# Hybrid encoder block on one core: w_out's second parts on VectorE, a slot table for each choice, and weight splits and the last normed row in other places around the last tile's routing

## The chip, the core and the metric

The kernel runs as one program on one core of a Trainium2 chip. The metric is the device time of one execution in microseconds (us); several executions are timed and their median is taken. The engines of a core are TensorE (PE in the profile, its weight loads PEld), VectorE (DVE), ScalarE (ACT), GpSimd (POOL) and SyncE (SP), each with an instruction queue that runs in order. Engines wait for one another and for DMA transfers through semaphores. DMA is issued from SyncE in most places, from ScalarE in some, and indirect DMA (rows by a list of indices) from GpSimd.

## What is computed

One layer over 2048 tokens of width 1024, all in float32:

```python
h = rmsnorm(x, mix_norm_g)
z = h @ w_in                                   # 512 + 512 + 2 * 1024 columns
y_f = fourier_mix(z[:, :512]) @ w_fourier_out
y_s = glu(gelu(ssm_both_directions(z[:, 512:1024]))) @ w_ssm_out
gates = sigmoid(z[:, 1024:])
x = x + (gates[:, :1024] * y_f + gates[:, 1024:] * y_s) @ w_out
hn = rmsnorm(x, ffn_norm_g)
group  = top_1(softmax(hn @ wg + bg))          # of 8 groups
expert = top_2(hn @ we + be, inside group)     # of 8 experts in it
w      = p_group * softmax(the two logits)
x = x + sum over the 2 choices of w * (silu(hn @ w_gate[e]) * (hn @ w_up[e])) @ w_down[e]
out = rmsnorm(x, final_norm_g)
```

There are 64 experts with an inner width of 512; gate, up and down of one expert are 6 MB, read as six blocks of 1 MB.

## The kernel before

**Products in two parts.** A float32 product is made of three products of a shorter type. `split` (L50 to L54) writes a tensor as a high part, a ScalarE copy (L53), and a second part, the difference of the two, by default on VectorE (L54). `mm3` (L57 to L61) issues high by high, high by low and low by high into one PSUM tile.

**The stages.** First come the input norm and w_in, the Fourier and state-space branches and the gates (to about 735 us of the profile), then the mixing stage `stage_m` (to about 1131 us and, with the routing of the last tiles, to about 1180), then `stage_e` with the experts, `stage_o` for experts with more than 128 tokens (a loop of `tot` passes over a row list, `For_i(0, tot)`; with these inputs `tot` is 0) and `stage_z`.

**Order in the mixing stage.** The order of its instructions comes out of a list of due times. `unit(d, f)` emits PE work of planned length d, after all that has come due by then; `at(dt, f)` puts f on the list dt after the present planned time; `flush` empties the list. A step's place in an engine's queue is thus set by these numbers.

The stage has blocks of 256 tokens. For each block b it makes the GLU (`glu`, tile names pglu, yr, y_h, y_l), then `merge` (L1265 and on): for each of 8 feature blocks, PE forms `pso` (y_s @ w_ssm_out) in a PSUM pool of three buffers that the GLU shares; VectorE multiplies it by its gate and adds the Fourier part (L1273, L1274, into gt_l); ScalarE copies the result to mg_h, and VectorE subtracts into mg_l (L54). `out_half` then forms merged @ w_out for half a tile of 128 tokens (tile `po`) and adds it to x (L1305, x_l). `w_out` itself is loaded in six pieces, four of one 128-row slice and two of two slices (`places`, L1392), into buffers that are still unused (raw_hn, raw_hnT, two raw_x_l, raw_mg_h, raw_mg_l), and split at times of their own (L1395): ScalarE makes the high part, and the second part of five pieces is made by GpSimd, of the last (k = 6) by VectorE.

**Norm and routing of a tile.** `norm` has four steps: the sum of squares on ScalarE (L1324, whose product goes into a buffer of the tag hn), its mean and a power of −1/2 on GpSimd (L1331, tile inv), a refinement step on VectorE (L1334 to L1337), and n4, which makes the normed row hn on VectorE (L1341) and stores it on SyncE (L1342). For tile 15 n4 is kept as `last_norm` and called at the end. `turn` transposes x, `logits` multiplies by the router weights (L1371), L1381 scales that to lg, and `route` is a generator whose steps choose the group and experts with small VectorE instructions and two tanh on ScalarE (L1557 r_th, L1580 r_td).

**The slot table.** Each (token, choice) gets a row in a table `tab` in DRAM: slot within the expert times 64 plus the expert; the row holds token number and weight. `clear_table` (L1505) zeroes the table early, with eight issues on SyncE during the stage before. The route steps scatter the entries of tiles 0 to 13 by indirect DMA from GpSimd (L1626), one instruction per tile and choice; as they write one tensor, each waits until the one before has landed. `load_table` (L1655) reads the first 128 slots of every expert to `tbm`, early in the last tile's routing. Tiles 14 and 15 don't go through DRAM there: PE multiplies one-hot matrices (r_a, built from r_pos, and r_b) into `ptab`, in PSUM, and `moe_open` adds `ptab` to `tbm` (L1704), makes the indices `ix` (L1751) and issues the gathers of the first three experts' rows of hn from DRAM (L1755). Their scatters follow later, for the overflow loop.

**Weights of the experts.** Blocks of 1 MB go into a ring of raw buffers (seven, two more, and two more after the last tile, `moe_weights` and `moe_pairs`). `split_h(n)` makes block n's high part on ScalarE (L1690, w_h), `split_l(n)` its second part on VectorE (L1696, w_l); only then is the raw buffer free, and `load_more` issues the next loads. Before `moe_open`, blocks 0 to 3 get their high parts and block 0 its second part; `moe_open` makes the second parts of 1, 2 and 3 behind the gathers.

These are the lines of the last tiles:

```python
at(-1.9, self.split_h, 0)
at(0.0, self.split_l, 0)
rs[15] = route(15, 1)
at(1.1, self.split_h, 1)
...
self.flush()
for _ in range(3):
    rs[15]()
self.last_norm()
```

## Time and profile before

Three executions took 2399.49, 2400.45 and 2407.3 us; the median is 2400.45. The profiled execution took 2403.95 us, of which the span of the profile is 2402.1.

| | busy, us | share of the span | instructions |
|---|---|---|---|
| TensorE products (PE) | 2264.6 | 94% | 11770 |
| TensorE weight loads (PEld) | 1911.2 | 80% | 11770 |
| VectorE (DVE) | 1928.8 | 80% | 2720 |
| ScalarE (ACT) | 1378.8 | 57% | 1699 |
| GpSimd (POOL) | 428.3 | 18% | 364 |
| DMA | 630.96 MB | mean 263 GB/s | 201326 packets |

Shares are averages over stages of different kinds, so a stretch must be looked at by itself. In the views of the trace that follow, a row of the timeline holds the start in us from the beginning of the span, the duration, the engine, the line of the kernel, the operation and its tiles (out<-in), and in brackets how long the engine had been idle ahead of it and who ended that. A PE product of 512 columns takes about 0.39 us from start to end, but is pipelined with the next.

### The profile page before, as it was taken

What the parts mean: (1) busy time and instruction counts of PE and PEld (TensorE: products, weight loads), DVE (VectorE), ACT (ScalarE), POOL (GpSimd) and SP (SyncE); (2) the same over time, 40 slices, a digit from 0 to 9 for tenths busy, and PEclk for the clock granted to TensorE, in tenths of its full rate; (3) what the DMA queues carried; (4) which work ended last, traced back from release to release, by engine and by line L of the source; (5) the groups of instructions that cost most, each with busy time, mean ns of one, the idle gap of its engine ahead of it and who ended that gap; (6) DMA issues with size and microseconds to landing.
All of it is one profiled execution on the core that took longest, in us unless ns stands there. A gap on an engine that the chain in (4) does not pass through costs nothing.

```text
span 2402.1 us, 32307 instructions
## 1 busy us (share of the span) xinstructions
PE 2264.6 (94%) x11770; PEld 1911.2 (80%) x11770; DVE 1928.8 (80%) x2720; ACT 1378.8 (57%) x1699; POOL 428.3 (18%) x364
## 2 busy tenths in 40 slices
PE   6999899999999999999699997999999999999995
PEld 6997678887887899997588886888888887777773
DVE  7876779988964566566799997999999998888877
ACT  4443235545543222221488886888888877777773
POOL 2224500000001000111122121211212112211132
PEclk9999999999999999999799999999999999999998
DMA  5555644364436534435799997999999999999975
GB/s 198 185 185 198 243 150 144 95 205 153 136 103 197 171 106 140 133 103 209 269 357 377 387 377 306 396 373 380 373 382 381 374 371 372 374 373 375 370 282 203
DMA packets 201326, 630.96 MB, mean 263 GB/s; under 512 B 29065, under 2 KB 100747, under 8 KB 150476
## 3 DMA queue, kind: packets, MB, share of 16 engines
q1 hardware_dynamic: 173068, 578.27, 64.7%
q0 software_dynamic: 20912, 39.10, 6.2%
q10 hardware_dynamic: 7184, 11.51, 1.5%
q8 instruction: 93, 1.52, 0.2%
q14 instruction: 69, 0.57, 0.1%
HBM read 552.28 MB, written 109.58 MB: 276 GB/s over the span
## 4 chain that ended last, share of the span: by engine, by line
PE 34%; DMA 26%; DVE 20%; issue 13%; ACT 4%; POOL 2%; SPq 1%; DVEq 0%; POOLq 0%; ACTq 0%
DMA raw<-in_w_e 16%; DVE w_l L1696 9%; DMA x<-xg,ix 6%; PE pg L59 4%; PE pg L61 3%; PE pg L60 3%; PE po L59 2%; PE po L61 2%; PE po L60 2%; PE pso L60 1%; PE pso L61 1%; PE pso L59 1%; POOL oh L1987 1%; PE pl L1371 1%; ACT xg L1797 1%
## 5 line engine op out<-in xcount | busy, mean ns | idle before, releaser
L1696 DVE TENSOR_TENSOR w_l<-raw,w_h 128x2048 fp32r<-128x2048 f32 x384 | 862.3, 2284 | 22.8 <-ACT w_h L1690 22.3
L1690 ACT CAST w_h<-raw 128x2048 fp32r<-128x2048 f32 x384 | 732.6, 1913 | 246.7 <-DMA raw<-in_w_e 88.0
L59 PE MATMUL pgu<-w_h,xT_h 128*128 128x512 f32 x1024 | 407.2, 398 | 12.2 <-issue 12.2
L60 PE MATMUL pgu<-w_l,xT_h 128*128 128x512 f32 x1024 | 401.7, 392 | 9.5 <-DVE w_l L1696 9.5
L61 PE MATMUL pgu<-w_h,xT_l 128*128 128x512 f32 x1024 | 400.9, 392 | 0.0
L1761 POOL DMA_INDIRECT x<-xg,ix x62 | 99.2, 1600 | 890.7 <-ACT xg L1797 859.4
L60 PEld LDWEIGHTS pgu<-w_l,xT_h 128*128 128x128 f32 x1024 | 193.5, 189 | 54.2 <-DVE w_l L1696 15.8
L59 PEld LDWEIGHTS pgu<-w_h,xT_h 128*128 128x128 f32 x1024 | 193.4, 189 | 51.1 <-issue 12.4
L61 PEld LDWEIGHTS pgu<-w_h,xT_l 128*128 128x128 f32 x1024 | 192.8, 188 | 41.6 <-DVE xT_l L1773 0.2
L59 PE MATMUL pg<-hk_h,wg_h 128*128 128x512 f32 x512 | 207.1, 405 | 8.4 <-ACT gt_t L836 8.3
L59 PE MATMUL py<-w_h,aT_h 128*128 128x512 f32 x512 | 205.6, 402 | 1.9 <-ACT aT_h L1771 1.9
L61 PE MATMUL pg<-hk_h,wg_l 128*128 128x512 f32 x512 | 201.7, 394 | 1.9 <-DVE wg_l L54 1.9
L60 PE MATMUL pg<-hk_l,wg_h 128*128 128x512 f32 x512 | 201.3, 393 | 0.0
L61 PE MATMUL py<-w_h,aT_l 128*128 128x512 f32 x512 | 200.3, 391 | 0.4 <-DVE aT_l L1773 0.4
L60 PE MATMUL py<-w_l,aT_h 128*128 128x512 f32 x512 | 200.2, 391 | 0.0
L1773 DVE TENSOR_TENSOR aT_l<-pst,aT_h 128x512 fp32r<-128x512 f32 x64 | 44.3, 691 | 96.2 <-ACT aT_h L1771 96.2
L59 PEld LDWEIGHTS pg<-hk_h,wg_h 128*128 128x128 f32 x512 | 97.3, 190 | 29.5 <-ACT gt_t L836 9.0
L61 PEld LDWEIGHTS pg<-hk_h,wg_l 128*128 128x128 f32 x512 | 97.4, 190 | 23.8 <-DVE wg_l L54 2.8
L61 PEld LDWEIGHTS py<-w_h,aT_l 128*128 128x128 f32 x512 | 96.6, 189 | 21.4 <-DVE aT_l L1773 0.9
L60 PEld LDWEIGHTS pg<-hk_l,wg_h 128*128 128x128 f32 x512 | 97.5, 190 | 19.7
L59 PEld LDWEIGHTS py<-w_h,aT_h 128*128 128x128 f32 x512 | 96.6, 189 | 20.0 <-ACT aT_h L1771 2.1
L60 PEld LDWEIGHTS py<-w_l,aT_h 128*128 128x128 f32 x512 | 96.7, 189 | 18.0
(534 smaller groups left out, 4613.8 us busy)
## 6 DMA issues: line engine op xcount, KB each, us to landing
raw<-in_w_e SPq DMA_DIRECT2D x376, 1024.0 KB
wg_raw<-in_w_g SPq DMA_DIRECT2D x32, 512.0 KB
hTh<-hp_h SPq DMA_DIRECT2D x8, 1024.0 KB
hTl<-hp_l SPq DMA_DIRECT2D x8, 1024.0 KB
hk_h<-hTh SPq DMA_DIRECT2D x16, 512.0 KB
hk_l<-hTl SPq DMA_DIRECT2D x16, 512.0 KB
yf<-yt SPq DMA_DIRECT2D x16, 512.0 KB
gt_y<-yf SPq DMA_DIRECT2D x32, 256.0 KB
```

The lines of the kernel that those rows point to most:

```text
L59: mm(out, a.h, b.h, start=start, stop=False)
L60: mm(out, a.h, b.l, start=False, stop=False)
L61: mm(out, a.l, b.h, start=False, stop=stop)
L1371: nc.tensor.matmul(pl[:, t % 2], hT[:, k], self.rw[:, k], start=k == 0, stop=k == KD - 1)
L1690: self.nc.scalar.copy(self.ws[n].h, self.raws[n][0])
L1696: self.nc.vector.tensor_tensor(out=w.l, in0=raw, in1=w.h.bitcast(F32), op=OP.subtract)
L1761: self.nc.gpsimd.indirect_dma_start(out=self.x2, out_offset=bass.IndirectOffsetOnAxis(ap=ix[:, e : e + 1], axis=0), in_=r, in_offset=None, ...
L1773: self.nc.vector.tensor_tensor(out=xT.l[:, k0 : k0 + 4], in0=ps, in1=xT.h[:, k0 : k0 + 4].bitcast(F32), op=OP.subtract)
L1797: self.nc.scalar.activation(r[:, 512 * n : 512 * n + 512], yo[n], AF.Copy, scale=tb[:, e, 1:2])
L1987: nc.gpsimd.tensor_scalar(ohs[n][:, t, q], self.iota, col[:, q, 2 * n + t : 2 * n + t + 1], None, op0=OP.is_equal)
```

## The change

Four edits. The second parts of all pieces of w_out are made on VectorE. The slot table becomes two (`tabs`), one for each choice, both cleared and both loaded, and added on VectorE ahead of `ptab`; the overflow loop reads both. In the routing of the last tiles, block 0's high part comes after the start of tile 15's route instead of ahead of it; its second part moves into `moe_open`, as the first of three, and block 3's goes behind the first transposes of `stage_e`. The last normed row is made and stored ahead of the last two steps of tile 15's route instead of behind them.

```diff
--- before.py
+++ after.py
@@ -1392,7 +1392,7 @@
         places = [(0, 1, mr, "hn"), (1, 1, mr, "hnT"), (2, 1, mr, "x_l"), (3, 1, mr, "x_l"), (4, 2, p2, "mg_h"), (6, 2, p2, "mg_l")]
         for k, n, pool, tag in places:
             at(1.7 * k if n == 1 else 7.8 + 1.05 * k, lambda a: load_w(*a[:-1], **a[-1]), ("w_out", k, pool, tag, n, {"bufs": 2} if tag == "x_l" else {}))
-            at(8.6 + 1.46 * (k + n), split_w, "w_out", wo, k, V if k == 6 else GP)
+            at(8.6 + 1.46 * (k + n), split_w, "w_out", wo, k)
         at(14.6, load_x, 0)
         at(14.6, load_x, 1)
         at(16.0, SP.dma_start, self.g2, i["ffn_norm_g"].broadcast_to([P, D]))
@@ -1470,16 +1470,17 @@
         at(0.3, self.load_more)
         unit(0.9, logits, 15, range(4, 8))
         unit(1.0, rs[14])
-        at(-1.9, self.split_h, 0)
-        at(0.0, self.split_l, 0)
         rs[15] = route(15, 1)
+        at(1.0, self.split_h, 0)
         at(1.1, self.split_h, 1)
         at(4.0, self.split_h, 2)
         at(4.1, self.split_h, 3)
         self.flush()
-        for _ in range(3):
+        rs[15]()
+        self.last_norm()
+        for _ in range(2):
             rs[15]()
-        self.last_norm()
+        self.nc.vector.tensor_tensor(out=self.tb, in0=self.tb, in1=self.tb2, op=OP.add)
         lx.close()
         self.late = rs[14], rs[15]
         self.moe_open()
@@ -1505,12 +1506,13 @@
     def clear_table(self):
 
         nc, SP, dr = self.nc, self.nc.sync, self.dr
-        self.tab = dr.tile([T * 64, 2], F32, name="tab")
+        self.tabs = [dr.tile([T * 64, 2], F32, name=f"tab{k}") for k in range(2)]
         emp = self.s_tmp.tile([P, 512], F32, name="emp", tag="sga")[:, 0:256]
         nc.gpsimd.memset(emp, 0.0)
-        ev = self.tab.rearrange("(a p b) f -> a p (b f)", p=P, b=P)
-        for a in range(T * 64 // P // P):
-            SP.dma_start(ev[a], emp)
+        for tab in self.tabs:
+            ev = tab.rearrange("(a p b) f -> a p (b f)", p=P, b=P)
+            for a in range(T * 64 // P // P):
+                SP.dma_start(ev[a], emp)
     ROUTE_STEPS = 7
 
     def route(self, t0, nt, lg, inv, late=False):
@@ -1624,7 +1626,7 @@
             for k in range(2):
                 yield
                 nc.gpsimd.indirect_dma_start(
-                    out=self.tab, out_offset=bass.IndirectOffsetOnAxis(ap=si[:, k, t : t + 1], axis=0), in_=ent[:, t, k], in_offset=None)
+                    out=self.tabs[k], out_offset=bass.IndirectOffsetOnAxis(ap=si[:, k, t : t + 1], axis=0), in_=ent[:, t, k], in_offset=None)
 
 
     def moe_weights(self):
@@ -1654,7 +1656,9 @@
 
     def load_table(self):
         self.tb = self.ep1.tile([P, 64, 2], F32, name="tbm")
-        self.nc.sync.dma_start(self.tb, self.tab[0 : P * 64].rearrange("(s e) f -> s e f", e=64))
+        self.tb2 = self.ep1.tile([P, 64, 2], F32, name="tb2")
+        for tb, tab in zip((self.tb, self.tb2), self.tabs):
+            self.nc.sync.dma_start(tb, tab[0 : P * 64].rearrange("(s e) f -> s e f", e=64))
 
     def next_raw(self):
 
@@ -1705,7 +1709,7 @@
         self.ix = self.slots(self.tb, 64, self.mr, "r_sel")
         for s in range(3):
             self.gather(self.ix, s, self.xgs[s])
-        for n in (1, 2, 3):
+        for n in (0, 1, 2):
             self.split_l(n)
 
     def moe_psum(self):
@@ -1837,6 +1841,7 @@
 
         turned(xgs[0], KD, "xT", xT, 0)
         self.flush()
+        self.split_l(3)
 
         def gate_up(s):
             for q in range(2):
@@ -1916,7 +1921,7 @@
         xg = self.mr.tile([P, D], F32, name="xo", tag="hn")
         row = self.row
         tot = nc.values_load(row[0:1, 0, 2:3], min_val=0, max_val=32)
-        tabv = self.tab.rearrange("(s e) f -> s e f", e=64)
+        tabv = [tab.rearrange("(s e) f -> s e f", e=64) for tab in self.tabs]
         raws, marks = zip(*self.loop_raws)
         w = Pair(raws[3], raws[4])
         both = raws[2].rearrange("p (q k j) -> p q k j", q=2, k=KD)
@@ -1924,8 +1929,10 @@
         with tc.For_i(0, tot) as j:
             er = nc.values_load(row[0:1, bass.ds(j, 1), 0:1], min_val=0, max_val=63)
             br = nc.values_load(row[0:1, bass.ds(j, 1), 1:2], min_val=0, max_val=T - 128)
-            tb = self.ep1.tile([P, 1, 2], F32, name="tbo")
-            nc.sync.dma_start(tb, tabv[bass.ds(br, P), bass.ds(er, 1)])
+            tb, tb2 = (self.ep1.tile([P, 1, 2], F32, name=n) for n in ("tbo", "tbo2"))
+            for t, tv in zip((tb, tb2), tabv):
+                nc.sync.dma_start(t, tv[bass.ds(br, P), bass.ds(er, 1)])
+            nc.vector.tensor_tensor(out=tb, in0=tb, in1=tb2, op=OP.add)
             ix = self.slots(tb, 1, self.ep1, "ixo")
             src = i["w_e"][bass.ds(er, 1)].rearrange("o q h p n -> (o q) h p n")
```

On VectorE, in the merge of block 0, this is what stood in a row before, from the last step of the GLU on (gt_l is the gated sum, mg_l its second part):

```order
L1250 SCALAR_TENSOR_TENSOR yr<-pglu,yr 128x256
L54 TENSOR_TENSOR y_l<-yr,y_h 128x256
L1273 SCALAR_TENSOR_TENSOR gt_l<-gt_l,pso 128x256
L1274 SCALAR_TENSOR_TENSOR gt_l<-mf_l,gt_l 128x256
L54 TENSOR_TENSOR mg_l<-gt_l,mg_h 128x256
L1273 SCALAR_TENSOR_TENSOR gt_l<-gt_l,pso 128x256
L1274 SCALAR_TENSOR_TENSOR gt_l<-mf_l,gt_l 128x256
L54 TENSOR_TENSOR mg_l<-gt_l,mg_h 128x256
```

And this is what stands there now, from the same GLU step on:

```order
L1250 SCALAR_TENSOR_TENSOR yr<-pglu,yr 128x256
L54 TENSOR_TENSOR y_l<-yr,y_h 128x256
L1273 SCALAR_TENSOR_TENSOR gt_l<-gt_l,pso 128x256
L1274 SCALAR_TENSOR_TENSOR gt_l<-mf_l,gt_l 128x256
L54 TENSOR_TENSOR w_out_l<-raw_hn,w_out_h 128x1024
L54 TENSOR_TENSOR mg_l<-gt_l,mg_h 128x256
L1273 SCALAR_TENSOR_TENSOR gt_l<-gt_l,pso 128x256
L1274 SCALAR_TENSOR_TENSOR gt_l<-mf_l,gt_l 128x256
L54 TENSOR_TENSOR mg_l<-gt_l,mg_h 128x256
L54 TENSOR_TENSOR w_out_l<-raw_hnT,w_out_h 128x1024
```

The first two pieces of w_out stand between block 0's gate and its second part, and behind block 1's second part. The next two (raw_x_l) stand the same way ahead of the second parts of blocks 3 and 4, the fifth (raw_mg_h, 128x2048) ahead of that of block 6; the sixth was on VectorE already.

On GpSimd, around the norm of tile 14 the scatters of tiles 10 to 12 stood like this before, all into one table (inv_10506 is the power of tile 13's norm, inv_10986<-mv_10984 that of tile 14's; r_ent_10469 are the entries of tiles 10 and 11, r_ent_10765 those of tile 12, r_ent_10951 of tile 13):

```order
L1626 DMA tab_3899<-r_ent_10469,r_si_10789 131072x2 x2
L1331 TENSOR_TENSOR inv_10506<-mv_10827,mhalf_63 128x1
L1626 DMA tab_3899<-r_ent_10469,r_si_10789 131072x2
L1626 DMA tab_3899<-r_ent_10765,r_si_10905 131072x2
L1626 DMA tab_3899<-r_ent_10469,r_si_10789 131072x2
L1626 DMA tab_3899<-r_ent_10765,r_si_10905 131072x2
L1331 TENSOR_TENSOR inv_10986<-mv_10984,mhalf_63 128x1
L1626 DMA tab_3899<-r_ent_10951,r_si_11070 131072x2 x2
```

Now the same place reads as follows, with tab0 for the first choice and tab1 for the second (inv_10515 is tile 13's, inv_10995<-mv_10993 tile 14's; the entries are r_ent_10478, r_ent_10774 and r_ent_10960):

```order
L1628 DMA tab0_3899<-r_ent_10478,r_si_10798 131072x2
L1628 DMA tab1_3900<-r_ent_10478,r_si_10798 131072x2
L1331 TENSOR_TENSOR inv_10515<-mv_10836,mhalf_63 128x1
L1628 DMA tab0_3899<-r_ent_10478,r_si_10798 131072x2
L1628 DMA tab0_3899<-r_ent_10774,r_si_10914 131072x2
L1628 DMA tab1_3900<-r_ent_10478,r_si_10798 131072x2
L1628 DMA tab1_3900<-r_ent_10774,r_si_10914 131072x2
L1331 TENSOR_TENSOR inv_10995<-mv_10993,mhalf_63 128x1
L1628 DMA tab0_3899<-r_ent_10960,r_si_11079 131072x2
L1628 DMA tab1_3900<-r_ent_10960,r_si_11079 131072x2
```

The order of the scatters is unchanged; between the powers of tiles 13 and 14 two go to tab0 and then two to tab1, where all four went to the same table.

On VectorE, at the end of the routing of tile 15 and the opening of the expert stage, before:

```order
L1600 TENSOR_TENSOR r_b<-r_oe,r_ent 128x256
L1609 TENSOR_TENSOR r_pick<-r_oe,pr 128x128
L1610 TENSOR_REDUCE r_pos<-r_pick 128x2
L1614 TENSOR_SCALAR r_a<-iota,r_pos 128x128 x2
L1619 SCALAR_TENSOR_TENSOR r_ek<-r_pos,r_ek 128x2
L1620 CAST r_si<-r_ek 128x2
L1622 TENSOR_TENSOR msum<-msum,r_m 128x64
L1341 SCALAR_TENSOR_TENSOR hn<-x_l,inv,g_7177 128x1024
L1704 TENSOR_TENSOR tbm<-tbm,ptab 128x128
L1751 TENSOR_SCALAR ix<-tbm 128x64
L1696 TENSOR_TENSOR w_l<-raw,w_h 128x2048 x3
L1773 TENSOR_TENSOR xT_l<-pst,xT_h 128x512 x2
```

And now, from the same instruction (r_b) on:

```order
L1602 TENSOR_TENSOR r_b<-r_oe,r_ent 128x256
L1341 SCALAR_TENSOR_TENSOR hn<-x_l,inv,g_7186 128x1024
L1611 TENSOR_TENSOR r_pick<-r_oe,pr 128x128
L1612 TENSOR_REDUCE r_pos<-r_pick 128x2
L1616 TENSOR_SCALAR r_a<-iota,r_pos 128x128 x2
L1621 SCALAR_TENSOR_TENSOR r_ek<-r_pos,r_ek 128x2
L1622 CAST r_si<-r_ek 128x2
L1624 TENSOR_TENSOR msum<-msum,r_m 128x64
L1483 TENSOR_TENSOR tbm<-tbm,tb_11220 128x128
L1708 TENSOR_TENSOR tbm<-tbm,ptab 128x128
L1755 TENSOR_SCALAR ix<-tbm 128x64
L1700 TENSOR_TENSOR w_l<-raw,w_h 128x2048 x3
```

The normed row hn moved from behind the msum row to a place behind r_b, the add of the two tables came in ahead of the add of `ptab`, and the three second parts behind ix are those of blocks 0, 1 and 2, where they were those of 1, 2 and 3. Further up, the single w_l row between tile 14's msum and lg is gone. On ScalarE the high part of block 0 stood ahead of r_th (L1557) of tile 15 and that of block 1 behind it; now both stand behind it, ahead of r_td (L1580). On SyncE the load of the second table stands behind that of the first, and two weight loads instead of three stand between them and the store of the last hn.

## The prediction, made before the changed kernel ran

> **What bounds the kernel now.** I read the page first, then what TensorE (PE) waited for in each stage, then the timeline of the places found. A wait row names who waits, for whom, us in total, times, longest; a window row its bounds and length, the busy time of PE, its weight loads, DVE, ACT and POOL, the granted PE clock, the DMA share and GB/s.
>
> ```profile
> span 2402.1 us, 32307 instructions
> PE pglu L59 <- DVE gt_l L1273: 6.1, 2, 4.5
> PE pso L59 <- DVE gt_l L1273: 3.4, 2, 1.7
> 795.00:1131.00 336.00, 335.33 (x2144) 303.34 (x2143) 197.53 (x675) 84.74 (x191) 34.97 (x41) 1.00 0.42 136
> PE pst L1769 <- DMA x_l<-hn,ix: 12.4, 1, 12.4
> PE pr L1604 <- DVE r_ent L1593: 4.8, 1, 4.8
> PE ptt L1361 <- DVE x_l L1305: 4.8, 2, 3.8
> 1300.00:1400.00 100.00, 100.00 (x478) 83.22 (x477) 92.92 (x64) 81.07 (x68) 18.62 (x10) 1.00 1.00 381
> 2100.00:2200.00 100.00, 96.42 (x452) 78.32 (x451) 87.92 (x59) 75.23 (x63) 18.85 (x11) 1.00 1.01 373
> PE pgu L59 <- issue: 12.2, 1, 12.2
> ```
>
> The kernel is a chain of PE-bound stretches with two holes. Where the mixing stage begins (735 to 805 us) PE waits 9.5 us for VectorE (DVE). From 795 to 1131 us it works 335.33 of 336 us, so whatever the first hole gives back reaches the second. There (1131 to 1170 us, the routing of the last tiles) it waits 22 us in three rows. Behind it the expert stage is PE-bound (100 of 100 us) and only later starved by DMA (96.42 of 100 at DMA share 1.01). Does an earlier start survive that late bound? The last row answers: at the loop for overflowing experts, near 1470 us, PE stands 12.2 us while the weight ring refills, and what follows starts from a full ring, whenever that is. I carry gains to the end one for one.
>
> **First hole: w_out's second parts.** GpSimd (POOL) computes five of the six.
>
> ```profile
> 766.03 0.42 DVE L1273 SCALAR_TENSOR_TENSOR gt_l<-gt_l,pso 128x256 f32<-128x256 f32 x1 [0.59 <-PE pso L61]
> 766.86 2.40 POOL L54 TENSOR_TENSOR w_out_l<-raw_hn,w_out_h 128x1024 fp32r<-128x1024 f32 x1 [388.39 <-DMA raw_x_l<-in_w_out]
> 770.81 0.43 DVE L54 TENSOR_TENSOR mg_l<-gt_l,mg_h 128x256 fp32r<-128x256 f32 x1 [0.47 <-ACT mg_h L53]
> 772.50 2.05 DVE L54 TENSOR_TENSOR mg_l<-gt_l,mg_h 128x256 fp32r<-128x256 f32 x1 [0.47 <-ACT mg_h L53]
> 784.66 4.53 DVE L54 TENSOR_TENSOR mg_l<-gt_l,mg_h 128x256 fp32r<-128x256 f32 x1 [0.90 <-ACT mg_h L53]
> 789.57 0.58 PE L59 MATMUL pglu<-yp_h,w_glu_h 128*128 128x256 f32 x1 [4.53 <-DVE gt_l L1273]
> 790.00:795.00 5.00, 5.00 (x25) 5.00 (x25) 3.23 (x4) 3.07 (x5) 0.00 (x0) 0.52 0.54 158
> 794.83 0.39 PE L59 MATMUL po<-w_out_h,mg_h 128*128 128x512 f32 x1
> 750.64 1.22 DVE L54 TENSOR_TENSOR w_so_l<-raw_y_h,w_so_h 128x1024 fp32r<-128x1024 f32 x1
> 792.53 2.29 DVE L54 TENSOR_TENSOR w_out_l<-raw_mg_l,w_out_h 128x2048 fp32r<-128x2048 f32 x1 [1.33 <-ACT w_out_h L53]
> ```
>
> A 0.43 us DVE instruction lasts 2.05 or 4.53 us while POOL runs beside it. Undisturbed, one block of the merge costs DVE 772.50 − 770.81 = 1.69 us, 0.47 of it idle behind ScalarE (ACT). Now the five instructions stand in DVE's own row: four of 128x1024 at about 1.14 us from start to start (1.22 less the overlap of 0.08 seen between neighbours), one of 128x2048 at 2.2. Three of the small ones fall into the idle 0.47, so each delays by 0.67, 2.0 together. The one behind block 1 waits some 0.6 us for its ACT copy first: 1.75. The large one waits for ACT's 1.9 us copy: 2.4, net of its idle gap. The first operation of block 7, which releases the PSUM buffer of the third glu block, thus starts at 766.03 (the first block's, unchanged) + 7 × 1.69 + 6.15 = 784.0, and PE, some 0.4 us later, at 784.4 instead of 789.57. Two glu blocks are left. Before, they took 5.26 us at a clock of 0.52; at full clock 2.7, with 0.3 us of waiting 3.0. The first w_out product comes at 787.4 instead of 794.83: **7.4 us**. PE's idle gap shrinks from 4.53 to about 2.6 us, but does not go; I charge 1.2 us for one slow clock window of 3.4 us with some chance, and take **6.2**. The ends are 7.6 (no slow window, the ACT waits hidden) and 4.0 (two slow windows as before and a late weight load ahead of DVE).
> On the clock, the Trainium skill ("TensorE: Matmul & The Clock Gate", Part 1) says that the array falls to half rate after an idle window of about 3.4 us, so a gap of 2.6 us would cost nothing and the sum would gain 1.2 us more. No gap of that length is in this trace.
>
> **Second hole: the scatters into the slot table.** Both choices of every tile go into one DRAM table, and each scatter waits for the landing of the one ahead.
>
> ```profile
> 1117.35 0.97 POOL L1626 DMA_INDIRECT tab<-r_ent,r_si  x1 [6.52 <-DVE r_oh L1541]
> 1123.63 0.96 POOL L1626 DMA_INDIRECT tab<-r_ent,r_si  x1 [5.30 <-DMA tab<-r_ent,r_si]
> 1129.01 0.96 POOL L1626 DMA_INDIRECT tab<-r_ent,r_si  x1 [4.42 <-DMA tab<-r_ent,r_si]
> 1130.60 0.16 DVE L1334 TENSOR_TENSOR mt<-inv 128x1 f32<-128x1 f32 x1 [9.45 <-POOL inv L1331]
> 1130.53 0.39 PE L61 MATMUL po<-w_out_h,mg_l 128*128 128x512 f32 x1
> 1134.01 0.69 DVE L1305 SCALAR_TENSOR_TENSOR x_l<-po,x_l 128x512 f32<-128x512 f32 x1
> 1136.70 0.20 DVE L1562 TENSOR_SCALAR r_den<-r_th 128x8 f32<-128x8 f32 x1 [0.61 <-ACT r_th L1557]
> ```
>
> The power instruction of tile 14's norm (L1331) was wanted at 1121.1, where DVE began its 9.45 us of waiting, and stood behind three scatters that waited 6.5, 5.3 and 4.4 us (the first named after DVE, but the landing came last). The order rows of the change show what is left: two scatters to one table, then two to the other, so the third no longer waits for the second. Two waits remain, about 7 and 6 us, and they begin 1.7 us earlier, as the first need not wait for the scatter ahead of it. The power instruction then runs at about 1124.2. DVE's 3.4 us of work behind it ends near 1128.3, before PE ends the first half of tile 15 (1130.53 + 0.39 = 1130.92). What is late next is PE itself: the residual add moves from 1134.01 to 1130.97, **3.0 us**. Tile 14's normed row is then long stored, so ACT's square, which reuses its buffer, and the tanh behind it are no longer late: **0.6**.
>
> **The moved split and the moved row.**
>
> ```profile
> 1143.16 1.99 PE L1371 MATMUL pl<-rw,hnT 128*128 128x72 f32 x8 [0.32 <-DVE hnT L1149]
> 1146.45 0.29 DVE L1381 SCALAR_TENSOR_TENSOR lg<-pl,inv,rb 128x72 f32<-128x72 f32 x1
> 1147.17 0.21 ACT L1557 ACTIVATE r_th<-r_th 128x8 f32<-128x8 f32 x1 [3.35 <-DVE r_th L1556]
> 1149.84 3.68 ACT L1690 CAST w_h<-raw 128x2048 fp32r<-128x2048 f32 x2
> 1150.45 0.15 DVE L1589 TENSOR_TENSOR r_td<-r_td,r_pg 128x1 f32<-128x1 f32 x1
> 1153.50 1.28 DVE L1341 SCALAR_TENSOR_TENSOR hn<-x_l,inv,g 128x1024 f32<-128x1024 f32 x1
> 1154.81 2.60 DMA hn<-hn
> 1158.65 7.87 DMA x_l<-hn,ix
> DMA to landing us min/median/max: 4.9/10.2/12.1
> ```
>
> Weight block 0's second part (2.2 us on DVE) leaves the place ahead of lg. Late next is PE's logit product, done at 1145.15: gain 1146.45 − 1145.15 = 1.3 at the slow clock that it had, 2.4 at full; I take **1.7**. ACT now runs two casts in a row (3.68 us) ahead of the second tanh of tile 15, which was free after one: DVE's r_td (L1589) comes 3.97 us behind the first tanh at 1147.17 instead of 3.28: **−0.7**. The normed row (hn) now follows r_b, 1.7 us earlier, so its store lands at 1155.7 instead of 1157.4. Behind it r_pick slips by 0.9 and one added 128x128 add comes (0.3, partly under the wait for the table product): the index is ready at 1155.8 instead of 1155.2, which is now the last to come. The gather left 1.24 us behind its last input, so **+1.65**. In front of its data stands one weight load less, since block 0 is freed later: 7.87 us falls towards the 4.9 that the fastest such gather took; I take 6.9, **+1.0**. Nothing waits for the moved second parts: the first expert needs them 13 us later, and DVE is idle for 6.6 us before its first transpose; block 3's stands behind the transposes and is used three blocks on. Sum: 3.0 + 0.6 + 1.7 − 0.7 + 1.65 + 1.0 = **7.25**, from 3 (only the routing's own wait shrinks) to 9.5 (full clock, gather at 4.9).
>
> **At no cost: the second table's clearing.**
>
> ```profile
> 378.54 4.67 SPq L1513 DMA_DIRECT2D tab<-emp  x8
> 383.94 9.12 SPq L831 DMA_DIRECT2D gt_y<-yf  x2
> 396.96 1.29 DVE L838 SCALAR_TENSOR_TENSOR gt_t<-gt_t,gt_y 128x512 f32<-128x512 f32 x2
> ```
>
> Eight more issues keep SyncE 4.7 us. Queued behind are a gate weight and gt_y; gt_y's first is read at 396.96, 13 us after its issue, and the second waited for a free buffer anyway. If that cover went, DVE would wait up to 4.7 us; from 0 to −4.7, and by the 13 us I take 0. The second table's load (0.85 us like the first's) stands on SyncE some ten us ahead of the store of hn: 0. The loop's body is longer, but with no overflow it does not run.
>
> **The sum** is made in the profiled execution, 2403.95 us with its span of 2402.1: 6.2 + 7.25 = 13.45 less is 2390.5. The median of the runs shown is 3.5 us below that execution, so the forecast is 2400.45 − 13.45 = **2387.0**.
>
> **Rivals.**
> One: DVE becomes the bound of the first merge, a w_out load lands late, and the 2.6 us gap still trips the clock twice. For it: DVE is in order, so the wait for ACT's copy, which POOL took before, now holds up the merge. Then the first hole returns 4.0 and less: 2400.45 − 3 − 7.25 = 2390.2.
> Two: the last tile's chain stays bound elsewhere, by the clock or by the gather behind weight loads; only 3 of 7.25 come: 2391.3.
> Three: two tables, but no two scatters beside each other; the landing of the second starts where the first ends. Then L1331 comes at about 1128.3, DVE is ready at 1132.3, and 2 us are lost: 2389. The Trainium skill ("DMA: Bandwidth & Descriptors", "Issuing engines are not separate DMA queues") says that concurrent starts save little beyond the issue, which would be this case. Against it, in this trace:
>
> ```profile
> 1134.26 2.17 DMA tab<-r_ent,r_si
> ```
>
> with the weights out of the way a landing takes 2.17 us, so the 5 to 7 us are traffic that two scatters can share.
> Four, slower: the pause of 12.2 us at the overflow loop. Its body gains a load and an add, the code of every engine changes there, and no row says what ends that pause ("issue"). If it grew beyond 12.2 + 13.45 = 25.7 us the kernel would be slower; at three times its length, 2411. Against it: only the body changes.
>
> **How the numbers follow.** A measurement of this kernel can tell about 0.3%, 7.2 us. The forecast, both holes smaller by 10 to 17 us (2383 to 2391), gets 0.64; rival one 0.12, two 0.10, three 0.05, four 0.04; 0.05 for more than 17 us. Faster by over 0.3% means below 2393.2: the forecast, the larger gain and most of one to three, 0.82. Within 0.3%: the rest of these and a disturbed run, 0.14; slower 0.04. The range takes in rivals one to three and the ends of the terms (4.0 + 3.0 = 7 less, with a us or two for the clearing, up to 17 to 20 more): 2379 to 2395.
>
> **What would show it.** In the profile after: the mg_l rows near 770 us all at 0.43; PE's longest wait for gt_l near 2.6 instead of 4.5; the first w_out product 6 to 7 us earlier; L1331 of tile 14 within 4 us of DVE's call; PE's wait of 3.8 for x_l below 1; the first gather about 13 us earlier. I am wrong if DVE waits for w_out copies in the merge, if the pause at the loop grows, or if PE waits more for weights behind 2000 us than before.

## The result, and the profile after

The changed kernel took 2390.59 us (median of five executions, 2385.87 to 2391.65); beside it the kernel before took 2403.75 (median of five). The ratio is 0.9943, its 95% interval 0.9929 to 0.9958: 0.57% faster, 13.2 us by the medians. From the 2400.45 of the earlier runs 2387.0 had been forecast. The profiled execution took 2391.65 us, 12.3 less than that of before; 13.45 had been forecast.

First the first hole. These rows are what TensorE waited for between 735 and 805 us in the changed kernel (who, for whom, us in total, times, longest):

```profile
PE pglu L59 <- DVE gt_l L1273: 2.9, 3, 1.8
PE pso L59 <- ACT y_h L53: 1.0, 2, 0.7
PE pso L60 <- DVE y_l L54: 0.9, 1, 0.9
```

The 9.5 us of waiting for gt_l are 2.9, and the longest wait is 1.8 instead of 4.5. The timeline of VectorE and TensorE there shows why:

```profile
765.89 1.22 DVE L54 TENSOR_TENSOR w_out_l<-raw_hn,w_out_h 128x1024 fp32r<-128x1024 f32 x1
767.03 0.42 DVE L54 TENSOR_TENSOR mg_l<-gt_l,mg_h 128x256 fp32r<-128x256 f32 x1
782.78 0.41 DVE L1273 SCALAR_TENSOR_TENSOR gt_l<-gt_l,pso 128x256 f32<-128x256 f32 x1
783.25 0.39 PE L59 MATMUL pglu<-yp_h,w_glu_h 128*128 128x256 f32 x1 [1.78 <-DVE gt_l L1273]
786.48 0.40 PE L59 MATMUL po<-w_out_h,mg_h 128*128 128x512 f32 x1
```

The second part of a block (mg_l) lasts 0.42 us where it lasted up to 4.53; the price is the w_out row of 1.22 ahead of it. The first w_out product comes at 786.48 instead of 794.83.

Now the second hole, on GpSimd and VectorE (in brackets how long the engine was idle, and for whom):

```profile
1106.80 0.97 POOL L1628 DMA_INDIRECT tab<-r_ent,r_si  x1 [6.49 <-DVE r_den L1564]
1108.08 0.96 POOL L1628 DMA_INDIRECT tab<-r_ent,r_si  x1 [0.31 <-issue]
1114.67 0.96 POOL L1628 DMA_INDIRECT tab<-r_ent,r_si  x1 [5.64 <-DMA tab<-r_ent,r_si]
1115.66 0.57 POOL L1331 TENSOR_TENSOR inv<-mv,mhalf 128x1 f32<-128x1 f32 x1
1116.26 0.16 DVE L1334 TENSOR_TENSOR mt<-inv 128x1 f32<-128x1 f32 x1 [3.48 <-POOL inv L1331]
```

Two waits of about 6 us are left of three; between the scatters to different tables there are 0.31 us, and both are under way at once, as they start 1.28 us apart and a landing took 2.17 in the trace of before even with the weights out of the way. VectorE's wait for the power of tile 14's norm is 3.48 us instead of 9.45. What TensorE waited for between 1120 and 1185 us:

```profile
PE pst L1773 <- DMA x_l<-hn,ix: 12.5, 1, 12.5
PE pr L1606 <- DVE r_ent L1595: 4.6, 1, 4.6
...
PE ptt L1361 <- DVE x_l L1305: 1.0, 1, 1.0
```

The wait of 3.8 us for the residual add is gone; the longest, for the first gather, is as long as before (12.5 against 12.4).

**A ledger by position.** Several executions of one kernel differ by 5 us and more, and part of that arises ahead of any edit: the first gate instruction stands at 294.50 us in the profile of before, and 0.5 to 5.5 us earlier in the others. So this document compares stretches within a profile. Four instructions bound them: VectorE's first GLU product, its first of the third token block, ScalarE's tanh of the first expert and of the last. In the profile of before and then in that of the changed kernel they stand at

```profile
757.65 0.42 DVE L1250 SCALAR_TENSOR_TENSOR yr<-pglu,yr 128x256 f32<-128x256 f32 x1 [4.67 <-ACT pglu L1249]
839.21 0.42 DVE L1250 SCALAR_TENSOR_TENSOR yr<-pglu,yr 128x256 f32<-128x256 f32 x1 [2.01 <-ACT pglu L1249]
1176.88 0.59 ACT L1830 ACTIVATE a<-pgu 128x512 f32<-128x512 f32 x1
2322.03 0.62 ACT L1830 ACTIVATE a<-pgu 128x512 f32<-128x512 f32 x1
```

```profile
756.71 0.42 DVE L1250 SCALAR_TENSOR_TENSOR yr<-pglu,yr 128x256 f32<-128x256 f32 x1 [5.12 <-ACT pglu L1249]
830.85 0.42 DVE L1250 SCALAR_TENSOR_TENSOR yr<-pglu,yr 128x256 f32<-128x256 f32 x1 [2.01 <-ACT pglu L1249]
1163.47 0.59 ACT L1834 ACTIVATE a<-pgu 128x512 f32<-128x512 f32 x1
2311.05 0.61 ACT L1834 ACTIVATE a<-pgu 128x512 f32<-128x512 f32 x1
```

The first hole returned (839.21 − 757.65) − (830.85 − 756.71) = 7.4 us, the second 337.67 − 332.62 = 5.05, and the expert stage behind them took 2.4 back. The rest of the 12.3 us lies outside the four: 0.9 ahead of the first, 1.3 behind the last. The same sum for every run, in us gained against the profile of before; the last column is TensorE's wait for the first gather, 12.4 before:

| run | first hole | second hole | expert stage | wait for gather |
|---|---|---|---|---|
| changed kernel | 7.4 | 5.1 | −2.4 | 12.5 |
| changed, again (c_again) | 5.6 | 7.6 | −0.8 | 8.7 |
| changed, third time (c_third) | 6.2 | 8.7 | 0.6 | 9.1 |
| e1_wout | 7.2 | −1.6 | 1.3 | 13.2 |
| e2_tables | 0.5 | 2.4 | 1.3 | 14.0 |
| e3_moves | 0.2 | 3.7 | 0.7 | 8.8 |
| e4_nomoves | 7.3 | 3.7 | 0.8 | 12.6 |
| e5_rowback | 5.8 | 7.3 | −1.1 | 12.1 |
| e5b_splitback | 6.3 | 4.2 | 1.8 | 12.1 |
| e6_token | 7.5 | 9.1 | 1.2 | 6.5 |
| f4_gpclear | 7.3 | 7.7 | 1.3 | 9.2 |
| f2_noload | 6.2 | 7.9 | 0.0 | 8.8 |
| f1_best | 6.3 | 11.1 | 1.5 | 5.9 |

Each row is one execution, measured against one of the kernel before. How far such numbers carry is seen where nothing was edited: e2_tables and e3_moves give 0.5 and 0.2 in the first hole, e1_wout −1.6 in the second.

### The profile page after: what moved, and what is told of

Same layout as the page of the kernel before. It is cut to its first block, busy times and chain, and to the rows that moved or that the text cites. A ratio compares the mean times of both kernels' runs of the same rounds, so it can differ in the third digit from the quotient of the medians.

```text
span 2389.8 us, 32324 instructions
## 1 busy us (share of the span) xinstructions
PE 2260.4 (95%) x11770; PEld 1907.6 (80%) x11770; DVE 1926.5 (81%) x2726; ACT 1378.1 (58%) x1699; POOL 416.7 (17%) x359
## 5 line engine op out<-in xcount | busy, mean ns | idle before, releaser
L59 PE MATMUL pgu<-w_h,xT_h 128*128 128x512 f32 x1024 | 407.7, 398 | 12.7 <-issue 12.7
L1331 POOL TENSOR_TENSOR inv<-mv,mhalf 128x1 f32<-128x1 f32 x16 | 9.0, 562 | 661.1 <-DVE mv L1330 661.0
```

What stands on the lines that cost most here:

```text
L59: mm(out, a.h, b.h, start=start, stop=False)
L1331: GP.tensor_tensor(out=y, in0=v, in1=self.mhalf[:, :1], op=OP.pow)
```

## Experiments: one edit at a time

The first four runs take the change apart, on one chip, against 30 executions of the kernel before (median 2401.2).

**w_out alone.**

```diff
-            at(8.6 + 1.46 * (k + n), split_w, "w_out", wo, k, V if k == 6 else GP)
+            at(8.6 + 1.46 * (k + n), split_w, "w_out", wo, k)
```

> The kernel before with the first edit alone: all second parts of w_out on VectorE. Theory: the whole gain of the first hole is this edit's, 7.4 us at the residual adds from 817 us of before on, and it reaches the end unchanged: 6 to 8.5 us less than before. PE's longest wait for gt_l falls from 4.5 to about 1.8 us and no slow clock follows. Rival: what is gained there is lost again in the wait for the scatters, which were issued from GpSimd by the landing of earlier ones and not by PE: then under 4 us at the end.

It took 2395.47 us, ratio 0.9977 (0.9968 to 0.9986), 5.5 us less. The first hole returned 7.2; TensorE's longest wait for gt_l is 2.3, not 1.8. Some 1.6 us went in the second hole, but only 0.3 of it ahead of the last residual add. The power instruction (L1331) of tile 14 came 9.7 us sooner than before and the third block's first GLU product 10.1 us sooner, so the scatters' chain moved with TensorE nearly whole, and the rival does not hold. The other 1.3 us went between the first gather and the first tanh.

**Two tables alone**, with clearing, load, add and the loop's body:

```diff
-                    out=self.tab, out_offset=...
+                    out=self.tabs[k], out_offset=...
...
+        self.nc.vector.tensor_tensor(out=self.tb, in0=self.tb, in1=self.tb2, op=OP.add)
```

> The kernel before with the two tables alone (clearing, scatters, load, add, loop body). Theory: PE's wait of 3.83 us for the residual add (x_l, L1305) falls to nothing, and with it the slow clock that followed, 1.4 us: 5 us less at the last residual add; the added add of the tables costs 0.2; 4 to 6 us less at the end. Rival (two scatters do not run beside each other): 2 us or less. Second rival: the second table's clearing costs over 1 us at 396 us, and 3 to 4 us are left.

2396.37 us, ratio 0.9979 (0.997 to 0.9988), 5.0 us less by the times. The wait for the residual add is gone, as expected (1.0 us is left of 4.8). But in its profile only 2.4 us pass the second hole. By the start of the last residual add 5.1 had been won; then the store of the last row and the gather, in the chain of waits of this run, took

```profile
1147.41 3.15 DMA hn<-hn
1151.75 8.98 DMA x_l<-hn,ix
```

against 2.60 and 7.87 us before. Another 1.1 us went between the first transposes and the first tanh. Why store and gather took longer is not shown: the DMA's share in the four us around the store's landing was 0.45 here (1147 to 1151 us) and 0.44 before (1154 to 1158).

**The moved splits and row alone.**

```diff
-        at(-1.9, self.split_h, 0)
-        at(0.0, self.split_l, 0)
         rs[15] = route(15, 1)
+        at(1.0, self.split_h, 0)
...
-        for _ in range(3):
+        rs[15]()
+        self.last_norm()
+        for _ in range(2):
             rs[15]()
-        self.last_norm()
```

> The kernel before with the moved splits and the moved last row alone. Theory: lg of tile 15 comes 1.3 to 2.2 us earlier against the last residual add, r_td gives 0.7 back, and the first gather's data gives another 1 to 1.5 back: between 1 us less and no change at the end. Rival (the prediction's terms): 3.5 us less (1.7 - 0.7 + 1.65 + 1.0).

2396.34 us, ratio 0.999 (0.9981 to 0.9998), so 2.4 us less by the ratio (0.5 to 4.6), 4.9 by the medians; 3.7 in the second hole. The expectation, made from the first profile after, was too low, and the prediction's terms fit: the wait for the gather falls from 12.4 to 8.8 us.

**The change without the moves.**

> The changed kernel with the splits and the last row put back where they were: w_out on VectorE and two tables remain. Theory: the two add up, 11.5 to 13.5 us less than before, so within 1.5 us of the changed kernel. Rival (the prediction's terms for the moved parts): 3.5 us slower than the changed kernel.

2392.81 us, ratio 0.9974 (0.9962 to 0.9987). Its holes gave 7.3 + 3.7. The copies of the changed kernel stand at 0.9943 to 0.9951. That is 2.3 to 3.1 thousandths, or 5.5 to 7.5 us, though two of the three intervals still overlap with this one's; the second holes differ by 1.4 to 5.1. The profiled execution was the fastest of six, so the 10.9 us of its holes are more than the six show together (6.2 us less by the ratio). The moves are worth some 3.5 us, with a wide margin. Again the expectation failed and the prediction's terms fit better.

## Experiments: inside the second hole

The next four ran on one chip, against 15 executions of before (2400.59).

**The changed kernel again.**

> The changed kernel once more, unaltered, so that the next three can be compared with it on one chip. If the profiles tell the kernel and not the run, the first hole again gives 7.4 us (against the first GLU product) and the second, up to the first expert's tanh, 4 to 6 us; the wait for the first gather is again 12 to 13 us and its data again takes over 9 us from the issue. What differs from the first profile by more than 1 us is not to be explained by the code.

2388.05 us, ratio 0.9948 (0.9932 to 0.9965). The code is the same and the holes are not: 5.6 and 7.6 instead of 7.4 and 5.1. The sums, 13.2 and 12.5, differ by less. The first gather is where the expectation fails: 8.7 us of waiting instead of 12.5. The store of the last row, the gather and the first transposes in this run:

```profile
1140.63 0.33 SPq L1342 DMA_DIRECT2D hn<-hn  x1
1144.50 1.94 POOL L1759 DMA_INDIRECT x_l<-hn,ix  x1 [12.46 <-issue]
1151.43 1.94 PE L1773 MATMUL pst<-ident,x_l 128*128 128x128 f32 x8 [8.70 <-DMA x_l<-hn,ix]
```

and in the first profile of the changed kernel:

```profile
1137.74 0.33 SPq L1342 DMA_DIRECT2D hn<-hn  x1
1142.80 2.95 POOL L1759 DMA_INDIRECT x_l<-hn,ix  x1 [13.37 <-DVE w_l L1700]
1152.37 1.94 PE L1773 MATMUL pst<-ident,x_l 128*128 128x128 f32 x8 [12.54 <-DMA x_l<-hn,ix]
```

From store to gather 3.9 us against 5.1, from gather to transposes 6.9 against 9.6. The profile names w_l as what ended the wait in the second case, but that is only the last event ahead of the start: in c_again the gather starts 1.4 us behind ix (1143.08), in the middle of the first w_l. In both runs the first of the three second parts releases a weight buffer, and SyncE issues a weight load 2.5 us behind ix, in the first profile and then in c_again at

```profile
1142.65 4.69 SPq L1678 DMA_DIRECT2D raw<-in_w_e  x3
1145.54 4.70 SPq L1678 DMA_DIRECT2D raw<-in_w_e  x3
```

The gather leaves 1.15 us behind the store's landing. In c_again, where the store landed in 2.7 us, the gather went out 1.0 us ahead of that load; in the first profile, where by the same 1.15 us the store took 3.9, the gather went out 0.15 us behind it. That first execution was an unlucky one in this place; what made its store slow stays open.

**The row put back.**

```diff
-        rs[15]()
-        self.last_norm()
-        for _ in range(2):
+        for _ in range(3):
             rs[15]()
+        self.last_norm()
```

> The changed kernel with the last normed row put back behind the last two steps of tile 15's route. Theory: the row's store then goes out about 1.4 us later but meets a DMA that the weight loads have left by then, lands in 2.6 instead of 3.9 us, and the gather starts within 0.5 us of where it did: no change of the time. Rival (the prediction's term): the gather goes out about 1.5 us later, as do all that follow.

2390.39 us, ratio 0.996 (0.9944 to 0.9976): 2.3 us over c_again, with intervals that overlap. The profile decides. From lg of tile 15 to the gather, in these two rows of the run, it takes 13.3 us,

```profile
1131.35 0.29 DVE L1381 SCALAR_TENSOR_TENSOR lg<-pl,inv,rb 128x72 f32<-128x72 f32 x1
1144.67 1.81 POOL L1758 DMA_INDIRECT x_l<-hn,ix  x1 [14.47 <-issue]
```

where c_again needs 11.0 (lg at 1133.46), c_third 11.3, f2_noload 11.6 and the first profile 12.2. The rival holds: the moved row brings the gather 1.1 to 2.3 us forward. The second hole still returned 7.3 here, as the last residual add came 1.6 us sooner than in c_again (5.8 us won by then, against 4.2).

**The splits put back, the row left.** 

```diff
+        at(-1.9, self.split_h, 0)
+        at(0.0, self.split_l, 0)
         rs[15] = route(15, 1)
-        at(1.0, self.split_h, 0)
...
-        for n in (0, 1, 2):
+        for n in (1, 2, 3):
             self.split_l(n)
...
-        self.split_l(3)
```

> The changed kernel with the weight splits put back (block 0 ahead of lg, blocks 1 to 3 behind the gathers), the row left where the change put it. Theory: lg of tile 15 comes 2.2 us later against the residual add, r_td wins 0.7 back, the index and the store are 1.5 us later; the gather leaves 1 to 1.5 us later. Rival: the gather is held by the store's landing and by weight loads alone, and nothing changes.

2389.8 us, ratio 0.9964 (0.995 to 0.9978). The second hole returned 4.2 and the gather was waited for 12.1 us. This is lg, with block 0's second part ahead of it again:

```profile
1132.01 2.29 DVE L1701 TENSOR_TENSOR w_l<-raw,w_h 128x2048 fp32r<-128x2048 f32 x1
1134.21 0.29 DVE L1381 SCALAR_TENSOR_TENSOR lg<-pl,inv,rb 128x72 f32<-128x72 f32 x1
```

As the theory had it: against the last residual add, lg comes 1.9 to 2.2 us later than in the three copies of the changed kernel. The gather then leaves 13.2 us behind lg, as the row's store was slow to land, which is what the rival named:

```profile
1140.77 5.45 DMA hn<-hn
```

The wait falls to 9 us or less only with row and splits both moved, and then in all profiles but the first. The order of gather and released load goes with it. In the seven profiles in which a weight load was issued ahead of the gather (before, the first of the changed kernel, e1_wout, e2_tables, e4_nomoves, e5_rowback, e5b_splitback) the transposes start 7.2 to 9.6 us behind the gather; in the five in which the gather left 0.3 to 1.2 us ahead (c_again, c_third, e3_moves, f4_gpclear, f2_noload) 6.5 to 7.1; in the two with VectorE held, e6_token and f1_best, it left 3.7 us ahead, and they start after 4.3 and 4.4. That is a pattern over runs, not the result of an edit that changes nothing else.

**VectorE held for the first gather.** The third gather, issued with VectorE quiet, lasts 1.00 us on GpSimd both before and after; the first, beside the second parts, 1.91 and 2.95. In c_again, where the second parts still run, the third takes 1.88.

```diff
         for s in range(3):
             self.gather(self.ix, s, self.xgs[s])
+            if s == 0:
+                tok = self.mr.tile([P, 1], F32, name="mv")
+                self.nc.gpsimd.memset(tok, 0.0)
+        self.nc.vector.tensor_copy(self.mr.tile([P, 1], F32, name="mt"), tok)
```

> The changed kernel with VectorE held for the first gather: GpSimd writes one element behind the first gather, VectorE copies it ahead of the three second parts, so that neither those nor the weight loads that they release run while GpSimd writes the first gather's descriptors. Theory: that gather's 2.95 us on GpSimd fall to 1.0, its data lands in at most 7 instead of 9.4 us from the issue, and the first transposes come 2.5 to 4 us earlier; nothing waits for the second parts, which end about when the transposed rows are copied. 2 to 4 us less than the changed kernel. Rival: the data of the gather stands behind weight loads issued earlier, and nothing changes.

```profile
1139.84 1.08 POOL L1763 DMA_INDIRECT x_l<-hn,ix  x1 [12.52 <-issue]
1144.20 1.94 PE L1777 MATMUL pst<-ident,x_l 128*128 128x128 f32 x8 [6.48 <-DMA x_l<-hn,ix]
```

In GpSimd's and TensorE's timeline the gather's issue lasts 1.08 us, and the transposes start 4.4 us behind it instead of 6.9 or 9.6; the second gather, now beside the second parts, lasts 3.10 instead of 1.83. The second hole returned 9.1, hardly more than c_third's 8.7: 3.4 us were lost again between the first transposes and the first tanh, which lie 13.6 us apart instead of 10.2 before. The expectation that nothing waits for the second parts was wrong. TensorE waited 1.3 us for xT_l, which stands behind them on VectorE; where the rest went is not settled. The time, 2386.2 us, ratio 0.9949 (0.9932 to 0.9967), cannot be told from c_again's: executions from 2383.86 to 2391.39 hide a gain of 2 us.

## Experiments: the clearing, and two more

These ran on one chip, against nine executions of before (2401.16).

> The changed kernel a third time, beside the next three on one chip. The two holes together give 12 to 13.5 us again, shared between them as the slow clock falls (7.4 + 5.1 and 5.6 + 7.6 in the two profiles so far); the first gather takes between 6.8 and 9.4 us from issue to landing.

2388.71 us, ratio 0.9951 (0.9937 to 0.9964). Its holes gave 6.2 + 8.7, more than expected; the gather was waited for 9.1 us, and its data came within the range expected (the transposes start 7.1 us behind it).

**The second table cleared from GpSimd's queue.** In the first profile of the changed kernel, VectorE and TensorE waited between 385 and 420 us for

```profile
DVE t4a L936 <- DMA wg_raw<-in_w_g: 1.2, 1, 1.2
PE pg L61 <- DVE wg_l L54: 0.9, 1, 0.9
```

and the profile of before has no such rows. SyncE issued a gate weight behind sixteen clearing writes instead of eight:

```profile
376.94 8.77 SPq L1515 DMA_DIRECT2D tab<-emp  x16
385.75 0.44 SPq L804 DMA_DIRECT2D wg_raw<-in_w_g  x1
```

The run was built on the reading that this weight came late.

```diff
-                SP.dma_start(ev[a], emp)
+                (nc.gpsimd if tab is self.tabs[1] else SP).dma_start(ev[a], emp)
```

> The changed kernel with the second table cleared by eight issues from GpSimd's queue in place of SyncE's. Theory: the prediction's nought for the clearing was wrong; a gate weight queued on SyncE behind the clearing came late, VectorE waited 1.2 us (t4a, L936) and TensorE 0.9 us (wg_l) near 395 us. Without it the gates after 396 us lose nothing against those before, 1.2 to 1.6 us less than the changed kernel there, of which about 1 us reaches the end. Rival: the loss comes from the added megabyte itself, and stays.

Neither wait is left in f4_gpclear, as in e1_wout, which has one table; c_again, e2_tables and c_third have both, of 0.9 to 1.3 us. So it was not the megabyte. But it was not the gate weight either. These rows are VectorE's wait in c_third and, in the first profile, the next cast of a gate weight:

```profile
386.85 0.43 DVE L936 TENSOR_TENSOR t4a<-bb,pw_w 128x256 f32<-128x256 f32 x1 [1.33 <-DMA tab<-emp]
400.10 1.04 ACT L53 CAST wg_h<-wg_raw 128x1024 fp32r<-128x1024 f32 x1
```

The cast comes 14 us behind the issue of the weight, which was thus in time, and in f4_gpclear the weight goes out only 0.8 us sooner (384.95).

The instruction that waits, L936, reads no gate weight at all. It writes t4a, and the kernel gives t4a the same buffer (tag sga, of which there is one) as emp, the zeros that the clearing writes read. It can start when the last of them is done. c_again, c_third, e2_tables and f2_noload name these writes as what ended the wait; the first profile names another transfer that ended near then. With two queues the last write is issued 0.9 us earlier against the instruction ahead of L936, and no wait is left. TensorE's 0.9 us follow, as VectorE makes wg_l (409.53) later by what it had waited.

The time is 2385.45 us, ratio 0.9936 (0.9923 to 0.995), 3.3 us under c_third, with intervals that overlap. How much of the 1.2 us reaches the mixing stage is not settled: from 294 to 757 us executions of one kernel differ by more.

**The released loads held back.** The emission of the loads behind the three second parts was put off:

```diff
-            self.load_more()
+            if more:
+                self.load_more()
```

> The changed kernel with the three second parts in their place behind the gathers, but the weight loads that they release issued only behind the first transposes. It parts the two causes that holding VectorE removed together. If VectorE beside GpSimd is what makes the first gather slow, that gather still takes 1.9 to 2.95 us on GpSimd and its data still 6.8 to 9.4 us from the issue. If the released loads are, GpSimd's time stays but the data lands within 5.5 us of the issue.

This tells nothing apart. On SyncE nothing stands between, so the load waits for its buffer as before and goes out at 1142.24 us, 0.5 behind the gather. The run is one more copy of the changed kernel (2390.11 us, ratio 0.9948, 0.9934 to 0.9961; holes 6.2 + 7.9). Whether VectorE's reads beside GpSimd or the released loads stretch the gather is not settled by it. Its length on GpSimd is not what counts: in f4_gpclear the first gather's issue took 1.20 us, little more than the 1.08 with VectorE held, and the transposes still started 6.7 us behind it. That, and the order of gather and load above, speak for the loads; no run holds back the loads alone.

**Both together**, with two second parts behind the held gather and two behind the first transposes:

```diff
-        for n in (0, 1, 2):
+        for n in (0, 1):
             self.split_l(n)
...
         self.flush()
+        self.split_l(2)
         self.split_l(3)
```

> The changed kernel with the second table cleared from GpSimd's queue, VectorE held for the first gather, two second parts behind it and the other two behind the first transposes. Theory: the gather as with VectorE held alone (1.1 us on GpSimd, 4.2 from issue to landing), the 1.3 us that TensorE then waited for xT_l gone, the clearing's 1.2 us gone: 6 to 8 us less than the changed kernel. Rival: the weights come later by as much, and the end is DMA-bound: 2 us or less.

```profile
1139.62 1.09 POOL L1763 DMA_INDIRECT x_l<-hn,ix  x1 [12.52 <-issue]
1143.90 1.94 PE L1777 MATMUL pst<-ident,x_l 128*128 128x128 f32 x8 [5.94 <-DMA x_l<-hn,ix]
```

In its profile the second hole returned 11.1 us, the most of all: the gather wins 3.7 us up to the transposes, as with VectorE held alone, and now only 0.3 is lost again behind them. That execution took 2378.31 us. The other four took 2382.89 to 2390.63, the median is 2387.36, the ratio 0.9941 (0.9927 to 0.9954). That is 1.4 us under c_third and not the 6 to 8 expected. It beats the kernel before; that it beats the changed kernel is shown for the stretch in one profile, not for the time.

## Why the prediction was right, step by step

**First hole, 6.2 forecast.** Four profiles of the changed code (the three copies and f2_noload, whose edit moved nothing) gave 7.4, 5.6, 6.2 and 6.2; the mean is 6.4. The agreement of the sum, 13.45 against 13.7 in the mean of these four, is better than that of its terms, as the second hole shows. The count of VectorE's rows held: block 7's first operation was forecast at 784.0, which is 783.1 by the 0.94 us that the profile was ahead (757.65 − 756.71), and came at 782.78. The first w_out product was forecast at 787.4 − 0.94 = 786.5 and came at 786.48. TensorE's longest idle gap ahead of it was 1.8 us and not 2.6. VectorE waited 0.5 us for one w_out copy in the merge, for which the sum had allowed 0.6.

The uncertain term was the clock, 1.2 us "with some chance". Window rows of the changed kernel and then of c_again (PE busy, and the granted clock third from the end):

```profile
765.00:775.00 10.00, 10.00 (x73) 9.96 (x71) 8.30 (x16) 4.88 (x8) 0.00 (x0) 0.83 0.68 241
785.00:795.00 10.00, 10.00 (x50) 8.53 (x51) 6.09 (x10) 3.53 (x8) 0.00 (x0) 1.00 0.51 166
```

```profile
785.00:795.00 10.00, 10.00 (x47) 8.74 (x46) 6.32 (x11) 3.69 (x8) 0.00 (x0) 0.85 0.58 185
```

Each of the three copies has slow stretches here, though no wait is longer than 1.9 us. In the first profile the slow stretch lies where VectorE sets the pace anyway and costs nothing (7.4); in c_again one lies behind the last wait, where TensorE is the bound, and the hole returned 1.8 less (5.6). From the first GLU product to the first w_out product the prediction allows 29.75 us at full clock and 30.95 with its 1.2; the four profiles took 29.77, 31.48, 30.94 and 30.93. So the charge had the right size, and which execution pays it is chance. The rule that was weighed there, of the Trainium skill ("TensorE: Matmul & The Clock Gate", Part 1), half rate after an idle window of about 3.4 us, would have made these gaps free; 0.83 and 0.85 in these rows speak against reading it so. The prediction says that the trace of before had no gap to try this on. It had one of 2.54 us, ended at 1183.84, and in the four us behind it the clock was 0.59 (third from the end):

```profile
1184.00:1188.00 4.00, 4.00 (x13) 3.31 (x14) 3.18 (x3) 0.59 (x1) 0.00 (x0) 0.59 0.97 334
```

The same page of the Trainium skill, under "A second HAM failure mode: psum-queue depth-cycling", tells of a clock that oscillates with short idle spells; the 0.83 and 0.85 here, with no wait over 1.9 us, agree with that.

**Second hole, 7.25 forecast.** The four profiles gave 5.1, 7.6, 8.7 and 7.9; the mean is 7.3. Its stretches, from the first GLU product of the third block on, in us gained, beside the forecast terms; e3_moves has the moves without the tables:

| stretch up to | forecast | first | c_again | c_third | f2_noload | e3_moves |
|---|---|---|---|---|---|---|
| the last residual add | 3.6 | 5.4 | 4.2 | 5.7 | 4.6 | −0.5 |
| lg of tile 15 | 1.7 | 2.2 | 1.9 | 2.2 | 1.6 | 2.1 |
| the first gather | −0.7 + 1.65 | 0.0 | 1.2 | 0.9 | 0.6 | 1.3 |
| the first transposes | 1.0 | −1.6 | 1.1 | 0.9 | 1.5 | 0.9 |
| the first expert's tanh | 0 | −0.9 | −0.8 | −1.0 | −0.4 | −0.1 |

So the total is partly luck: the first row gives 1.4 more than forecast in the mean of the four, and the three last ones together 1.6 less. What the 0.4 to 1.0 us of the last row are stays open. The terms one by one:

- The scatters, 3.0 + 0.6. The power ran at 1115.66, which with the 8.36 us won by then (839.21 − 830.85) is 1124.0; 1124.2 had been forecast. The term itself was too small, by a misread row. The prediction takes the product at 1130.53 for the end of tile 15's first half and lets the residual add wait for it. But these rows, two of before and one of the changed kernel, show that the first half had ended at 1126.4:

```profile
1125.97 0.40 PE L61 MATMUL po<-w_out_h,mg_l 128*128 128x512 f32 x1
1134.75 0.66 PE L1361 MATMUL ptt<-ident,x_l 128*128 128x128 f32 x4 [3.83 <-DVE x_l L1305]
1122.40 0.60 PE L1361 MATMUL ptt<-ident,x_l 128*128 128x128 f32 x4
```

The products up to 1130.92 already belong to the second half. So the add, at 1119.68 + 8.36 = 1128.04, waits for VectorE alone, and TensorE's wait of 3.83 us goes whole. With it goes slow clock behind it: the last residual add came 3.6 to 5.8 us earlier in the runs with two tables.

- lg without the split ahead of it, 1.7: 1.6 to 2.2 in the four.
- The second tanh behind two casts, −0.7, and with the later index −1.3: −1.06 in all of them.
- The row and the gather, 1.65 + 1.0: the three others of the four bear it out (wait for the gather 8.7 to 9.1 instead of 12.4), as does e3_moves, and e5_rowback shows the row's part. The first profile, alone, does not. One step of the term failed: the index was not the last to come. The store's landing was, in all four, by 0.1 to 1.3 us, as it took 2.7 to 3.9 us where 2.60 had been assumed.

**The clearing, 0 forecast: wrong.** The prediction asked what is queued behind the clearing on SyncE, "a gate weight and gt_y", and neither was late. What it did not ask is who is next to use the buffer of zeros that the clearing reads: 1.2 us on VectorE and 0.9 on TensorE in the first profile, within the bounds given (0 to −4.7). How much of it reaches the end is not settled.

**Carried one for one.** TensorE's pause at the overflow loop:

```profile
PE pgu L59 <- issue: 12.7, 1, 12.7
PE pgu L60 <- DVE w_l L1700: 10.7, 15, 1.1
```

12.7 us instead of 12.2, and 11.0 to 12.7 over all runs, with one table read in the body or two: rival four does not occur. The second row, of 1450 to 2250 us, was 8.0 before: late waits for weights grew by 2.7 in this profile, and by 0.8 to 1.3 in the three others. They begin sooner; behind 2000 us, where the prediction had put its sign of being wrong, they are 8.6 to 9.1 in the four and 9.5 before. Over the four profiles the expert stage returned −2.4, −0.8, 0.6 and 0.0, about −0.7 in the mean. Gains arrive nearly whole.

**Rivals.** One (VectorE bound, first hole 4.0 or less) fell with the 5.6 to 7.5 us of every run that has the edit. Three (no two scatters at once) fell with the power at 1124.0 where it has 1128.3. Two, the gather behind weight loads, is what the first profile shows, at 5.1 instead of 3.

## What to carry to other kernels

When a path is shortened in front of a DMA, look for its gain behind that DMA too: of the 5.1 us that the two tables alone had won at the last residual add, 2.7 were gone at the first tanh, 1.6 of them up to the first transposes. For an insertion into a DMA queue, list every transfer behind it, and also the next user of each buffer that the new transfers read: here the one without slack was such a user. Where executions differ by more than an edit is worth, compare stretches between fixed instructions, in several profiles of the same code, before explaining a number.

## What was unexpected

- The first gather's issue on GpSimd lasts 1.08 us with VectorE held and 1.2 to 2.95 in the same place beside VectorE's 2.28 us subtractions.
- One profile of a kernel can mislead by 2 to 4 us in one place: the first gather was waited for 12.5 us in one and 8.7 to 9.1 in three others, where the holes together gave 12.5 and 13.2 to 15.0.
- The granted clock fell to 0.83 and 0.85 in 10 us near the first hole without any single wait over 1.9 us.
